# Two hybrid layers on one core: the second 512 columns of gate and up computed directly, the seven-product accumulators moved to one PSUM pool and read by ScalarE, other SBUF slots, the row sums of x ranked late

## The chip, the cores and the metric

The kernel runs on 1 core of one Trainium2 chip. The metric is the device time of one execution in microseconds (us). The kernel before has a median of 2263.99 us over 3 runs (2261.82 to 2264.88). Engines are named as in the profile: PE is TensorE, DVE VectorE, ACT ScalarE, POOL GpSimd, SP the queue that starts nearly all transfers.

## What is computed

Two layers over 256 tokens with a model width of 2048, in fp32. Each layer adds three things to x: a mixer (a state-space half and a latent-attention half), a cross-attention to a memory, and a gated MLP. The change lies in the MLP, with its norm in front:

```
h = rms_norm(x, ffn_norm_g[l])
x = x + swiglu(h, w_gate[l], w_up[l], w_down[l])
def swiglu(h, w_gate, w_up, w_down):
    return (jax.nn.silu(h @ w_gate) * (h @ w_up)) @ w_down    # 2048 -> 5632 -> 2048
```

## The kernel before, in words

**Exact products from two parts.** A weight arrives as a raw unit of 256 rows by 512 columns (512 KB, a tile of 128x1024). `split_w` makes two parts of it: `hi`, the raw number rounded to the fast fp32 format (a CAST, on ACT as a rule), and `lo`, the rest (a subtraction on DVE). The rows of x are split the same way. A product then takes three matmuls: x hi with weight lo, x hi with weight hi, x lo with weight hi. Nothing but these makes the work of DVE and ACT so large. All instructions are issued from one place, so the profile's rows all bear line 374, and tiles tell them apart.

**The MLP.** Its 5632 hidden columns are taken in eleven chunks of 512, in sections [0], [1,2], [3,4], and so on to [9,10]. For each chunk gate and up are computed, silu(gate) times up is formed in the tiles `gg`/`hh`, and it is turned by a transposing transfer (`split_T_dma`, `turn`) into the parts `hTh`, `hTl`. After each chunk of a section, `down` runs half of the output columns for the section before (48 or 96 matmuls), into `acc` tiles that `add_x` adds to x on DVE.

Chunk 0 is computed directly: `gemm` over the four quarters of the 2048 rows, for gate and then for up, 96 matmuls of 512 columns each, so 192. All other chunks go through `gate_up`. It combines the two token blocks, two parts of the rows and the pair gate/up as two-by-two block matrices and forms them with seven block products in place of eight (the quarter x1, rows 512 to 1023, stays direct). The products need sums of x's blocks (`s1` to `s4`, made once per layer in `seven_rows`) and sums of weights (`add(b11, b11, b12)` and such, on DVE; `plus` adds one more by an accumulating transfer on POOL's queue). In each chunk that is 7 times 18 plus 48 = 174 matmuls, 25 units to split where the direct way has 16, 10 sums of raw units on DVE and 2 accumulating transfers.

**Banks and slots.** The eight PSUM banks are two pools of four: `acc` (the gemms) and `tp` (transposes and small work). `gate_up` takes its first two accumulators, `q` and `f`, from `acc` and the other two, `cg` and `cu`, from `tp`; `down` takes its two per 512 output columns from `acc` too. In SBUF, 20 slots of the pool `w` hold raw, hi and lo units, 22 slots `b4` hold the parts of x, hT and their kin, 6 slots `s2` hold small tiles.

**Who sets the order.** Nothing is written to an engine at once. A recorder takes all instructions with a rank (place in the program plus `rec.bias`: smaller goes first), and `issue` then plays a list schedule with its own costs, engine by engine, picking the one that can start first and among those the lowest rank; slots are given out in that play as well. The chip runs the resulting order, each engine strictly in its own. Splits have a bias of -400, the sums `add` of -425, `add_x` none.

Of the kernel before, what the change touches and what calls it, by code (L numbers as in the profile page):

```python
# [17 lines left out]
P = 128  # L18
# [359 lines left out]
def hybrid_kernel(ctx: ExitStack, tc: tile.TileContext, const, vec, rows, x_in, x_tr, mem, mem_tr, positions, w_in, w_q_b,  # L378
# [110 lines left out]
    def load_unit(w, r0, c0, n, pieces=1):  # L489

        if not ahead and not asked:
            return ask(w, r0, c0, n, pieces)
        key = id(w), r0, c0
        while key not in asked or (ahead and len(asked) <= 2):
            first = ahead.pop(0)
            asked[id(first[0]), first[1], first[2]] = ask(*first, 512)
        return asked.pop(key)

    def load_raw(w, r0, c0, n, pieces=1):

        return [load_unit(w, r0 + 256 * h, c0, n, pieces) for h in range(2)]

    def ask(w, r0, c0, n, pieces=1):
        raw = wpool.tile([P, 2, n], F32, tag="w", name=nm("raw"), bufs=20)
        src = w[r0:r0 + 256, c0:c0 + n].rearrange("(k p) n -> p k n", p=P)
        for i in range(pieces):
            k = slice(2 // pieces * i, 2 // pieces * (i + 1))
            SP.dma_start(raw[:, k, :], src[:, k, :])
        return raw
# [116 lines left out]
    def norm_chunk_whole(j, ssx, g, by_dma=False):  # L626

        x_squares(j, ssx)
        xg = b4([P, 4, S], "xg")
        if by_dma:  # L630
            turn(lambda t: x[j][:, t, :], xg.rearrange("p b s -> p (b s)"))
            for b in range(4):
                copy(xg[:, b, :], xg[:, b, :], g[:, 4 * j + b:4 * j + b + 1])
            return xg
        for pair in range(2):
            ps = tp_tile().rearrange("p (b s) -> p b s", b=2)
            for i in range(2):
                b = 2 * pair + i
                for t in range(NT):
                    T.transpose(ps[:, i, t * P:(t + 1) * P], x[j][:, t, b * P:(b + 1) * P], ident)  # L640
                copy(xg[:, b, :], ps[:, i, :], g[:, 4 * j + b:4 * j + b + 1])
        return xg

    def seven_rows(xa, xb, n):


        a = {f"a{t + 1}{i + 1}": src[:, :, t * P:(t + 1) * P] for i, src in enumerate((xa, xb)) for t in range(NT)}
        if n == 4:
            sums = [b4([P, 2, 4, P], "xs") for _ in range(2)]
            tmp = [sums[i // 2][:, i % 2] for i in range(4)]  # L650
        else:
            sums = b4([P, 4, 2, P], "xs")
            tmp = [sums[:, i] for i in range(4)]
        out, room = {}, []
        for name in ("a11", "a12", "a22", "a21", "s1", "s2", "s3", "s4"):
            if name[0] == "s":
                a[name] = tmp[int(name[1]) - 1]
                do, u, v = {"s1": (V.tensor_sub, "a21", "a22"), "s2": (V.tensor_sub, "s1", "a11"),
                            "s3": (V.tensor_sub, "a11", "a21"), "s4": (V.tensor_add, "a12", "s2")}[name]
                do(a[name], a[u], a[v])  # L660
            if n == 4:
                d = b4([P, 2, 4, P], "x7", F32R)
            else:
                if not room:
                    both = b4([P, 2, 2, 2, P], "x7", F32R)
                    room = [both[:, 0], both[:, 1]]
                d = room.pop(0)
            copy(d[:, 0], a[name])
            V.tensor_sub(d[:, 1], a[name], d[:, 0].bitcast(F32))
            out[name] = d  # L670
        return out

    def load_T(src, j, g, name, pieces=1):
# [486 lines left out]
    def mem_T(l):  # L1160
# [10 lines left out]
        rec.after = None  # L1171
        return mT

    def add_x(j, accs):
        for t in range(NT):
            xs = x[j][:, t, :]
            V.tensor_add(xs, xs, accs[t])

    mixer_end, hidden_end = [None], [None]

# [120 lines left out]
            src = w[r0 + 256 * h:r0 + 256 * (h + 1), c0:c0 + 512].rearrange("(k p) n -> p k n", p=P)  # L1301
            G.dma_start(raw[h], src, accum_op=ALU.add)

    def add(out, a, b, do=V.tensor_add):
        rec.bias -= 425
        for o, u, v in zip(out, a, b) if isinstance(out, list) else [(out, a, b)]:
            do(o, u, v)
        rec.bias += 425

    def gate_up(wg, wu, c, x1, half, full, rstd):  # L1310

        c0 = 512 * c
        q, f = acc_tile(), acc_tile()
        cg, cu = tp_tile(), tp_tile()
        gg, uu = b4([P, NT, 512], "gg"), [s2([P, 512], "uu") for _ in range(NT)]  # L1320

        def product(acc, d, raw, start=False, stop=False):
            parts = split_w(raw)
            order = [(h, k, i) for h in range(len(parts)) for k, i in ((0, 1), (1, 1), (0, 0), (0, 2), (1, 0), (1, 2))]
            for m, (h, k, i) in enumerate(order):
                T.matmul(acc, d[:, i // 2, 2 * h + k, :], parts[h][i % 2][:, k, :], start=start and m == 0,
                         stop=stop and m == len(order) - 1, skip_group_check=True)

        b11 = load_raw(wg, 1024, c0, 512)
        product(q, full["a11"], b11, start=True)  # L1330
        h11 = load_unit(wg, 0, c0, 512)
        product(q, half["a11"], [h11])
        A.copy(gg[:, 0, :], q)

        b12 = load_raw(wu, 1024, c0, 512)
        add(b11, b11, b12)
        product(f, full["s1"], b11, start=True)
        h12 = load_unit(wu, 0, c0, 512)
        add(h11, h11, h12)
        product(f, half["s1"], [h11])  # L1340
        A.copy(uu[0], f)

        b22 = load_raw(wu, 1536, c0, 512)
        add(b11, b11, b22)
        add(b12, b12, b22)
        product(cu, full["s4"], b22, start=True)
        h22 = load_unit(wu, 256, c0, 512)
        add(h11, h11, h22)
        add(h12, h12, h22)
        product(cu, half["s4"], [h22])  # L1350
        product(q, full["s2"], b11)
        plus(b11, wg, 1536, c0)
        product(q, half["s2"], [h11])
        add(uu[0], uu[0], q, V.tensor_sub)

        b21 = load_raw(wg, 1536, c0, 512)
        product(cg, full["a12"], b21, start=True)
        h21 = load_unit(wg, 256, c0, 512)
        add(h11, h11, h21)
        product(cg, half["a12"], [h21])  # L1360
        product(q, full["s3"], b12)
        product(q, half["s3"], [h12])
        mm_chunk([cu, f], x1, load_w(wu, 512, c0, 512), 512, [False] * NT, [True, True], again=True)
        A.copy(uu[1], f)
        add(uu[1], uu[1], q, V.tensor_sub)
        add(uu[0], uu[0], cu)
        mm_chunk([cg, q], x1, load_w(wg, 512, c0, 512), 512, [False] * NT, [True, False], again=True)
        add(gg[:, 0, :], gg[:, 0, :], cg)
        A.activation(gg[:, 0, :], gg[:, 0, :], AF.Silu, scale=rstd[:, 0:1])

        product(q, full["a22"], b11)
        product(q, half["a22"], [h11], stop=True)
        A.activation(gg[:, 1, :], q, AF.Silu, scale=rstd[:, 1:2])
        for t in range(NT):
            V.scalar_tensor_tensor(gg[:, t, :], uu[t], rstd[:, t:t + 1], gg[:, t, :], op0=ALU.mult, op1=ALU.mult)
        return gg

    def ffn(l, xT, rstd):
# [18 lines left out]
        sections, before = [[0], [1, 2], [3, 4], [5, 6], [7, 8], [9, 10]], None  # L1397
        for sec in sections:
            for i, c in enumerate(sec):
                if c == 0:  # L1400
                    ahead.extend((w, r + h, 0) for w in (wg, wu) for r in FULL for h in (0, 256))
                else:
                    ahead.extend((w, r, 512 * c) for w, r in (
                        (wg, 1024), (wg, 1280), (wg, 0), (wu, 1024), (wu, 1280), (wu, 0), (wu, 1536), (wu, 1792),
                        (wu, 256), (wg, 1536), (wg, 1792), (wg, 256), (wu, 512), (wu, 768), (wg, 512), (wg, 768)))
                if before:
# [6 lines left out]
        for sec in sections:  # L1413
            hT = []
            for i, c in enumerate(sec):
                if c == 0:
                    xs = [lambda i, k, t: half[f"a{t + 1}{1 + k // 2}"][:, i, k % 2, :], x1]
                    xs += [lambda i, k, t, b=b: full[f"a{t + 1}{b}"][:, i, k, :] for b in (1, 2)]
                    ag = gemm(xs, wg, FULL, 0, 512)
                    hh = b4([P, NT, 512], "gg")  # L1420
                    for t in range(NT):
                        A.activation(hh[:, t, :], ag[t], AF.Silu, scale=rstd[:, t:t + 1])
                    au = gemm(xs, wu, FULL, 0, 512)
                    for t in range(NT):
                        V.scalar_tensor_tensor(hh[:, t, :], au[t], rstd[:, t:t + 1], hh[:, t, :], op0=ALU.mult,
                                               op1=ALU.mult)
                else:
                    hh = gate_up(wg, wu, c, x1, half, full, rstd)
                hc = chunk_T("hT")
                split_T_dma(hc, lambda t: hh[:, t, :], None, hh.rearrange("p t (u s) -> p (t u) s", s=S), (A, V))  # L1430
                hT.append(hc)
                if before:
                    n = DC // len(sec)
# [88 lines left out]
```

## Time and profile before

| | |
|---|---|
| median of 3 runs | 2263.99 us |
| the profiled execution | 2267.05 us, its span 2265.3 us |
| granted TensorE clock, mean | 0.997 |
| PE busy in the span | 2222.9 us (98%) |
| DVE / ACT busy | 1910.6 us (84%) / 1500.4 us (66%) |
| HBM read | 450.92 MB |

The MLP of the first layer runs on PE from about 434 to 1131 us, that of the second from about 1561 to 2262 us. In the page's 40 slices PE is below 9 tenths in two alone, which begin at 510 and 1642 us; DVE is at 9 or more tenths in most slices of the two MLPs.

### The profile page before, as it was taken

The numbers are of one execution on the slowest core, as the hardware profiler recorded it, in microseconds if no ns is written. First come the engines' busy times: TensorE is split into PE (matmuls) and PEld (weight loads), VectorE is DVE, ScalarE is ACT, GpSimd is POOL, SyncE is SP. The second block draws the span as 40 slices with busy tenths as digits, with TensorE's granted clock in tenths as the row PEclk, the third lists the DMA queues.
The fourth block names the chain that finished last, engine by engine and source line by source line (L and its number), as shares of the span: only waits on it lengthen the run. The fifth ranks groups of instructions, "written<-read, shape, count | busy, mean of one in ns | idle before, by whom it ended". The sixth has DMA issues, their size and how long they took to land.

```text
span 2265.3 us, 29133 instructions
## 1 busy us (share of the span) xinstructions
PE 2222.9 (98%) x10118; PEld 1845.7 (81%) x10118; DVE 1910.6 (84%) x2568; ACT 1500.4 (66%) x2183; POOL 93.0 (4%) x78
## 2 busy tenths in 40 slices
PE   9999999998999999999999999999989999999999
PEld 9878878787888888888898788887878888888787
DVE  7898876789998999999778888857899999999894
ACT  7768666766766666676666686657666667666762
POOL 0001000000000000000000010000000000000000
PEclk9999999999999999999999999999999999999999
DMA  9866496676777777787777665856767777777773
GB/s 319 236 193 186 142 284 196 187 212 197 239 224 212 229 232 235 228 247 226 194 230 223 172 177 171 244 185 182 219 201 226 232 220 213 236 231 226 239 234 138
DMA packets 374515, 487.96 MB, mean 215 GB/s; under 512 B 145376, under 2 KB 168544, under 8 KB 374368
## 3 DMA queue, kind: packets, MB, share of 16 engines
q1 hardware_dynamic: 363456, 465.13, 65.1%
q0 software_dynamic: 10912, 20.98, 5.5%
q8 instruction: 79, 1.29, 0.2%
q14 instruction: 68, 0.56, 0.1%
HBM read 450.92 MB, written 2.10 MB: 200 GB/s over the span
## 4 chain that ended last, share of the span: by engine, by line
PE 71%; DVE 6%; DMA 5%; issue 2%; ACT 1%; SPq 0%; DVEq 0%; ACTq 0%
PE acc L374 59%; PE tp L374 13%; DVE lo L374 3%; DMA raw<-in_w_up_dram 1%; DVE raw L374 1%; DMA ht<-hs 1%; ACT hi L374 1%; DVE x L374 1%; DMA raw<-in_w_xv_dram 0%; DMA raw<-in_w_out_dram 0%; DMA raw<-in_w_in_dram 0%; DVE uu L374 0%; DMA raw<-in_w_gate_dram 0%; SPq L374 0%; DVE hTl L374 0%
## 5 line engine op out<-in xcount | busy, mean ns | idle before, releaser
L374 ACT CAST hi<-raw 128x1024 fp32r<-128x1024 f32 (+3 forms) x996 | 1002.7, 1034 | 559.9 <-PE acc L374 223.4
L374 DVE TENSOR_TENSOR lo<-raw,hi 128x1024 fp32r<-128x1024 f32 (+3 forms) x998 | 1167.9, 1200 | 177.3 <-ACT hi L374 125.2
L374 PE MATMUL acc<-hi,x 128*128 128x512 f32 x1392 | 373.1, 392 | 0.0
L374 PEld LDWEIGHTS acc<-hi,x 128*128 128x128 f32 x1392 | 263.4, 189 | 55.4
L374 PE MATMUL acc<-hi,xTh 128*128 128x512 f32 (+1 forms) x768 | 289.3, 377 | 0.0
L374 PE MATMUL acc<-hi,xTl 128*128 128x512 f32 (+1 forms) x768 | 289.1, 376 | 0.0
L374 DVE TENSOR_TENSOR raw<-raw,raw 128x1024 f32<-128x1024 f32 x200 | 239.2, 1221 | 50.7 <-DMA raw<-in_w_up_dram 50.2
L374 PE MATMUL acc<-hi,hTh 128*128 128x512 f32 x704 | 273.9, 389 | 0.0
L374 PE MATMUL acc<-hi,hTl 128*128 128x512 f32 x704 | 273.9, 389 | 0.0
L374 PE MATMUL acc<-lo,x 128*128 128x512 f32 x696 | 214.8, 394 | 13.2 <-DVE x L374 13.2
L374 PE MATMUL acc<-lo,xTh 128*128 128x512 f32 (+1 forms) x768 | 211.7, 378 | 6.0 <-DVE uu L374 4.2
L374 PE MATMUL acc<-lo,hTh 128*128 128x512 f32 x704 | 191.2, 390 | 1.3 <-DVE lo L374 1.3
L374 PEld LDWEIGHTS acc<-lo,xTh 128*128 128x128 f32 x768 | 140.6, 188 | 31.3 <-DVE uu L374 6.8
L374 PEld LDWEIGHTS acc<-lo,x 128*128 128x128 f32 x696 | 131.1, 190 | 42.5 <-DVE x L374 14.9
L374 PEld LDWEIGHTS acc<-hi,xTh 128*128 128x128 f32 x768 | 144.8, 189 | 23.2 <-issue 0.7
L374 PEld LDWEIGHTS acc<-hi,xTl 128*128 128x128 f32 x768 | 144.7, 188 | 23.1 <-issue 0.7
L374 PEld LDWEIGHTS acc<-lo,hTh 128*128 128x128 f32 x704 | 131.8, 188 | 30.1 <-DVE lo L374 3.0
L374 PEld LDWEIGHTS acc<-hi,hTh 128*128 128x128 f32 x704 | 132.1, 188 | 27.5
L374 PEld LDWEIGHTS acc<-hi,hTl 128*128 128x128 f32 x704 | 132.1, 188 | 27.4
L374 PE MATMUL tp<-hi,x 128*128 128x512 f32 x480 | 128.6, 390 | 0.0
L374 DVE TENSOR_TENSOR x<-x,acc 128x512 f32<-128x512 f32 x128 | 83.5, 682 | 32.5 <-PE acc L374 32.4
L374 PEld LDWEIGHTS tp<-hi,x 128*128 128x128 f32 x480 | 90.1, 188 | 19.2
(306 smaller groups left out, 2781.7 us busy)
## 6 DMA issues: line engine op xcount, KB each, us to landing
raw<-in_w_gate_dram SPq DMA_DIRECT2D x176, 512.0 KB, 4.9
raw<-in_w_up_dram SPq DMA_DIRECT2D x176, 512.0 KB, 4.5
raw<-in_w_down_dram SPq DMA_DIRECT2D x176, 512.0 KB, 5.4
raw<-in_w_in_dram SPq DMA_DIRECT2D x80, 512.0 KB, 4.4
raw<-in_w_out_dram SPq DMA_DIRECT2D x64, 512.0 KB, 4.5
raw<-in_w_gate_dram POOLq DMA_DIRECT2D x40, 512.0 KB, 7.5
raw<-in_w_in_dram SPq DMA_DIRECT2D x46, 368.0 KB, 4.5
raw<-in_w_kv_b_dram SPq DMA_DIRECT2D x16, 512.0 KB, 3.9
```

The lines of the kernel that those rows point to most:

```text
L374: fn(*args, **kw)
```

## The change

Five edits. (1) Chunk 1 is computed directly like chunk 0, so `gate_up` runs 9 times in a layer. (2) In `gate_up` all four accumulators come from `tp`. ACT copies `q` out after the second and the third product that end in it, where DVE subtracted it from a copy of `f` made earlier; DVE then subtracts that copy from `f` in its bank. The product of `s4` with `b22` stands ahead of the two sums that read `b22`. (3) Other slots: `gg` and `hh` are two `s2` tiles each, the turned words go to a `b4` tile of their own (`whole`) and not back into `gg`, and the raw units of rows 0 to 255 (`h11`, `h12`) take `b4` slots and not `w` slots. (4) The four sums of x's blocks rank 300 later, and in `norm_chunk_whole` the transposes of a pair come before its two copies. (5) `add_x` gets the bias of -425. The diff, cut to its core:

```diff
-    def ask(w, r0, c0, n, pieces=1):
-        raw = wpool.tile([P, 2, n], F32, tag="w", name=nm("raw"), bufs=20)
+    def ask(w, r0, c0, n, pieces=1, other=False):
+        raw = b4([P, 2, n], "raw") if other else wpool.tile([P, 2, n], F32, tag="w", name=nm("raw"), bufs=20)
...
@@ seven_rows
         for name in ("a11", "a12", "a22", "a21", "s1", "s2", "s3", "s4"):
+            if name == "s1":
+                rec.bias += 300
...
+        rec.bias -= 300
         return out
...
     def add_x(j, accs):
         for t in range(NT):
             xs = x[j][:, t, :]
-            V.tensor_add(xs, xs, accs[t])
+            add(xs, xs, accs[t])
...
@@ gate_up
-        q, f = acc_tile(), acc_tile()
-        cg, cu = tp_tile(), tp_tile()
-        gg, uu = b4([P, NT, 512], "gg"), [s2([P, 512], "uu") for _ in range(NT)]
+        q, f, cg, cu = (tp_tile() for _ in range(4))
+        gg, uu = [[s2([P, 512], n) for _ in range(NT)] for n in ("gg", "uu")]
...
         product(f, half["s1"], [h11])
-        A.copy(uu[0], f)
 
         b22 = load_raw(wu, 1536, c0, 512)
+        product(cu, full["s4"], b22, start=True)
         add(b11, b11, b22)
         add(b12, b12, b22)
-        product(cu, full["s4"], b22, start=True)
         h22 = load_unit(wu, 256, c0, 512)
+        product(cu, half["s4"], [h22])
         add(h11, h11, h22)
         add(h12, h12, h22)
-        product(cu, half["s4"], [h22])
         product(q, full["s2"], b11)
         plus(b11, wg, 1536, c0)
         product(q, half["s2"], [h11])
-        add(uu[0], uu[0], q, V.tensor_sub)
+        A.copy(uu[0], q)
+        add(uu[0], f, uu[0], V.tensor_sub)
...
         product(q, half["s3"], [h12])
+        A.copy(uu[1], q)
         mm_chunk([cu, f], x1, load_w(wu, 512, c0, 512), 512, [False] * NT, [True, True], again=True)
-        A.copy(uu[1], f)
-        add(uu[1], uu[1], q, V.tensor_sub)
+        add(uu[1], f, uu[1], V.tensor_sub)
         add(uu[0], uu[0], cu)
         mm_chunk([cg, q], x1, load_w(wg, 512, c0, 512), 512, [False] * NT, [True, False], again=True)
...
@@ ffn
-                if c == 0:
+                if c < 2:
...
-                    ag = gemm(xs, wg, FULL, 0, 512)
-                    hh = b4([P, NT, 512], "gg")
+                    ag = gemm(xs, wg, FULL, 512 * c, 512)
+                    hh = [s2([P, 512], "gg") for _ in range(NT)]
...
-                split_T_dma(hc, lambda t: hh[:, t, :], None, hh.rearrange("p t (u s) -> p (t u) s", s=S), (A, V))
+                split_T_dma(hc, lambda t: hh[t], None, None, (A, V))
```

The first place is PE's queue in the first layer where the first half of `down` (`hTh`, `hTl` into `acc`) ends and the next `gate_up` begins with its product of `a11` (here the tile `x_841`) into `q`. Before (the next chunk is number 2):

```order
L374 MATMUL acc_5074<-hi_4984,hTl_4980 128x512
L374 MATMUL acc_5076<-hi_4984,hTh_4805 128x512
L374 MATMUL acc_5076<-hi_4984,hTl_4980 128x512
L374 MATMUL acc_5124<-lo_5027,x_841_4421 128x512 x2
L374 MATMUL acc_5124<-hi_5000,x_841_4421 128x512 x4
```

And now, at the same place of the program:

```order
L374 MATMUL acc_5049<-hi_4928,hTl_4798 128x512
L374 MATMUL acc_5057<-hi_4928,hTh_4786 128x512
L374 MATMUL acc_5057<-hi_4928,hTl_4798 128x512
L374 MATMUL tp_5087<-lo_4958,x_841_4404 128x512 x2
L374 MATMUL tp_5087<-hi_4946,x_841_4404 128x512 x4
```

What was `acc_5124`, a fifth tile on the four banks that `down` fills, is now `tp_5087` on a bank that `down` never uses.

The second place is DVE's queue around the same point, with the sums `x<-x,acc` of `add_x` that empty `down`'s banks (`x_215` and `x_302` are the first two column quarters of x). Before:

```order
L374 TENSOR_TENSOR raw_4952<-raw_4952,raw_5046 128x1024
L374 TENSOR_TENSOR raw_5002<-raw_5002,raw_5046 128x1024
L374 SCALAR_TENSOR_TENSOR gg_4733<-uu_4847,rx_y_4548,gg_4733 128x512
L374 TENSOR_TENSOR lo_5112<-raw_4991,hi_5102 128x1024
L374 TENSOR_TENSOR raw_4957<-raw_4957,raw_5096 128x1024
L374 TENSOR_TENSOR raw_5019<-raw_5019,raw_5096 128x1024
L374 SCALAR_TENSOR_TENSOR gg_4733<-uu_4959,rx_y_4548,gg_4733 128x512
L374 TENSOR_TENSOR x_215<-x_215,acc_5035 128x512
L374 TENSOR_TENSOR x_215<-x_215,acc_5037 128x512
L374 TENSOR_TENSOR x_302<-x_302,acc_5074 128x512
L374 TENSOR_TENSOR x_302<-x_302,acc_5076 128x512
```

And now:

```order
L374 TENSOR_TENSOR raw_4705<-raw_4705,raw_4972 128x1024
L374 SCALAR_TENSOR_TENSOR gg_4860<-acc_4862,rx_y_4377,gg_4860 128x512
L374 TENSOR_TENSOR lo_5023<-raw_4900,hi_5013 128x1024
L374 TENSOR_TENSOR raw_4936<-raw_4936,raw_4999 128x1024
L374 TENSOR_TENSOR raw_4900<-raw_4900,raw_4999 128x1024
L374 TENSOR_TENSOR x_215<-x_215,acc_5008 128x512
L374 TENSOR_TENSOR x_215<-x_215,acc_5011 128x512
L374 TENSOR_TENSOR lo_5059<-raw_4915,hi_5035 128x1024
```

The first pair of sums of x stood behind two rounds of weight sums and both products with up; it now stands behind one split and two weight sums, and the second pair no longer follows it at once.

The third place is PE's queue in the same `gate_up`, where the direct quarter (`xTh`, `xTl`) of up ends and that of gate goes on in `q`. Before, in chunk 2, two matmuls of the next `down` stand between:

```order
L374 MATMUL tp_5238<-hi_5320,xTh_4340 128x512
L374 MATMUL tp_5238<-hi_5320,xTl_4352 128x512
L374 MATMUL acc_5410<-lo_5383,hTh_4805 128x512
L374 MATMUL acc_5414<-lo_5383,hTh_4805 128x512
L374 MATMUL acc_5124<-lo_5333,xTh_4340 128x512 x2
L374 MATMUL acc_5124<-hi_5308,xTh_4340 128x512
```

And now, with `f` in `tp_5120`, `cu` in `tp_5157`, `cg` in `tp_5227` and `q` in `tp_5087`:

```order
L374 MATMUL tp_5157<-hi_5254,xTl_4391 128x512
L374 MATMUL tp_5120<-hi_5254,xTh_4383 128x512
L374 MATMUL tp_5120<-hi_5254,xTl_4391 128x512
L374 MATMUL tp_5227<-lo_5287,xTh_4383 128x512
L374 MATMUL tp_5087<-lo_5287,xTh_4383 128x512
L374 MATMUL tp_5227<-hi_5267,xTh_4383 128x512
```

The quarter for `cg` and `q` follows at once and takes both token blocks in turn, where before `cg` was done alone, then `q`. Over the whole program PE gets 36 more matmuls of 512 columns, DVE 18 fewer splits and 20 fewer sums of raw units, ACT 28 fewer casts, and POOL 4 fewer accumulating transfers. In the mixers and the output projections no engine's order changes.

## Rows read from the trace of the kernel before

**Rows 1.** The page, busy time of each engine over the span.

```profile
PE 2222.9 (98%) x10118; PEld 1845.7 (81%) x10118; DVE 1910.6 (84%) x2568; ACT 1500.4 (66%) x2183; POOL 93.0 (4%) x78
```

**Rows 2.** Stretches of both MLPs: length, busy us of PE, PEld, DVE, ACT, POOL, PEclk.

```profile
434.00:530.00 96.00, 94.83 (x424) 77.78 (x423) 84.74 (x95) 64.93 (x86) 4.20 (x3) 1.00 0.66 201
530.00:552.00 22.00, 16.36 (x61) 12.92 (x60) 17.87 (x19) 13.05 (x15) 1.98 (x2) 0.84 0.56 165
552.00:1131.00 579.00, 573.83 (x2518) 471.47 (x2517) 522.78 (x524) 388.33 (x438) 20.68 (x18) 1.00 0.75 227
1561.00:1657.00 96.00, 94.85 (x422) 77.34 (x422) 84.40 (x95) 64.72 (x85) 4.17 (x3) 1.00 0.66 202
1657.00:1679.00 22.00, 16.29 (x62) 12.97 (x61) 18.33 (x20) 13.12 (x15) 1.85 (x2) 0.84 0.57 163
1679.00:2262.00 583.00, 575.27 (x2522) 471.95 (x2520) 508.90 (x488) 369.98 (x404) 19.93 (x17) 1.00 0.72 222
```

**Rows 3.** PE's waits, first layer's MLP: for whom, total us, times, longest us.

```profile
PE acc L374 <- DVE x L374: 6.0, 2, 5.6
PE tp L374 <- DVE lo L374: 2.2, 4, 1.2
PE acc L374 <- DVE uu L374: 1.7, 3, 0.7
PE tp L374 <- DVE x L374: 1.2, 1, 1.2
```

**Rows 4.** PE's waits, second layer's MLP.

```profile
PE acc L374 <- DVE x L374: 7.2, 2, 5.7
PE tp L374 <- DVE lo L374: 2.6, 3, 1.2
PE acc L374 <- DVE uu L374: 2.5, 3, 1.3
```

**Rows 5.** PE in order of time, first layer: start, us, what, [idle before].

```profile
537.22 1.22 PE L374 MATMUL acc<-lo,x 128*128 128x512 f32 x2 [5.64 <-DVE x L374]
...
543.15 1.07 PE L374 MATMUL acc<-hi,x 128*128 128x512 f32 x4
```

**Rows 6.** The same place in the second layer.

```profile
1664.70 1.22 PE L374 MATMUL acc<-lo,x 128*128 128x512 f32 x2 [5.71 <-DVE x L374]
...
1669.68 0.63 PE L374 MATMUL acc<-lo,x 128*128 128x512 f32 x2
```

**Rows 7.** DVE in order of time during the first layer's wait.

```profile
533.55 2.36 DVE L374 TENSOR_TENSOR raw<-raw,raw 128x1024 f32<-128x1024 f32 x2
535.82 0.75 DVE L374 SCALAR_TENSOR_TENSOR gg<-uu,rx_y,gg 128x512 f32<-128x512 f32 x1
536.48 2.48 DVE L374 TENSOR_TENSOR x<-x,acc 128x512 f32<-128x512 f32 x4
```

**Rows 8.** The chain that ended last: start, us, what; a product's 18 matmuls.

```profile
604.86 4.08 PE acc L374 x18
```

**Rows 9.** Groups of the first MLP, DVE, by form: count, busy us, mean ns, idle before.

```profile
L374 DVE TENSOR_TENSOR lo<-raw,hi 128x1024 fp32r<-128x1024 f32 x347 | 408.7, 1220 | 26.8 <-ACT hi L374 17.4 <-PE acc L374 6.0 <-issue 1.1
L374 DVE TENSOR_TENSOR raw<-raw,raw 128x1024 f32<-128x1024 f32 x100 | 119.7, 1221 | 25.3 <-DMA raw<-in_w_up_dram 25.1
```

**Rows 10.** The same of ACT.

```profile
L374 ACT CAST hi<-raw 128x1024 fp32r<-128x1024 f32 x345 | 350.0, 1051 | 184.5 <-PE acc L374 98.6 <-DMA raw<-in_w_up_dram 34.7 <-DMA raw<-in_w_down_dram 22.6
```

**Rows 11.** SP in order of time, loads ahead of chunk 4.

```profile
629.82 2.59 SPq L374 DMA_DIRECT2D raw<-in_w_gate_dram  x3
...
639.24 3.00 SPq L374 DMA_TRANSPOSE ht<-hs  x1
```

**Rows 12.** PE in order of time, chunk 4's first product.

```profile
653.65 0.61 PE L374 MATMUL acc<-lo,x 128*128 128x512 f32 x2
```

**Rows 13.** The page, transfers: issuer, count, size, median us to landing.

```profile
raw<-in_w_gate_dram SPq DMA_DIRECT2D x176, 512.0 KB, 4.9
```

**Rows 14.** PE in order of time, one wait for the subtraction from `uu`, second layer.

```profile
1878.40 0.73 PE L374 MATMUL acc<-lo,xTh 128*128 128x512 f32 x2 [1.06 <-DVE uu L374]
```

More of the change, by code (lines that the diff above doesn't have):

```diff
@@ L495, in load_unit @@
             first = ahead.pop(0)
-            asked[id(first[0]), first[1], first[2]] = ask(*first, 512)
+            asked[id(first[0]), first[1], first[2]] = ask(*first[:3], 512, 1, first[3:])
         return asked.pop(key)
@@ L640, in norm_chunk_whole @@
                     T.transpose(ps[:, i, t * P:(t + 1) * P], x[j][:, t, b * P:(b + 1) * P], ident)
+            for i in range(2):
+                b = 2 * pair + i
                 copy(xg[:, b, :], ps[:, i, :], g[:, 4 * j + b:4 * j + b + 1])
@@ L1172, in mem_T, with add @@
         return mT
+    def add(out, a, b, do=V.tensor_add):
+        rec.bias -= 425
+        for o, u, v in zip(out, a, b) if isinstance(out, list) else [(out, a, b)]:
+            do(o, u, v)
+        rec.bias += 425
     def add_x(j, accs):
@@ L1302, in plus @@
             G.dma_start(raw[h], src, accum_op=ALU.add)
[L1304 to L1308, printed above, removed]
     def gate_up(wg, wu, c, x1, half, full, rstd):
         c0 = 512 * c
-        q, f = acc_tile(), acc_tile()
-        cg, cu = tp_tile(), tp_tile()
-        gg, uu = b4([P, NT, 512], "gg"), [s2([P, 512], "uu") for _ in range(NT)]
+        q, f, cg, cu = (tp_tile() for _ in range(4))
+        gg, uu = [[s2([P, 512], n) for _ in range(NT)] for n in ("gg", "uu")]
         def product(acc, d, raw, start=False, stop=False):
@@ L1332, in gate_up @@
         product(q, half["a11"], [h11])
-        A.copy(gg[:, 0, :], q)
+        A.copy(gg[0], q)
         b12 = load_raw(wu, 1024, c0, 512)
@@ L1362, in gate_up @@
         product(q, half["s3"], [h12])
+        A.copy(uu[1], q)
         mm_chunk([cu, f], x1, load_w(wu, 512, c0, 512), 512, [False] * NT, [True, True], again=True)
-        A.copy(uu[1], f)
-        add(uu[1], uu[1], q, V.tensor_sub)
+        add(uu[1], f, uu[1], V.tensor_sub)
         add(uu[0], uu[0], cu)
         mm_chunk([cg, q], x1, load_w(wg, 512, c0, 512), 512, [False] * NT, [True, False], again=True)
-        add(gg[:, 0, :], gg[:, 0, :], cg)
-        A.activation(gg[:, 0, :], gg[:, 0, :], AF.Silu, scale=rstd[:, 0:1])
+        add(gg[0], gg[0], cg)
+        A.activation(gg[0], gg[0], AF.Silu, scale=rstd[:, 0:1])
         product(q, full["a22"], b11)
         product(q, half["a22"], [h11], stop=True)
-        A.activation(gg[:, 1, :], q, AF.Silu, scale=rstd[:, 1:2])
+        A.activation(gg[1], q, AF.Silu, scale=rstd[:, 1:2])
         for t in range(NT):
-            V.scalar_tensor_tensor(gg[:, t, :], uu[t], rstd[:, t:t + 1], gg[:, t, :], op0=ALU.mult, op1=ALU.mult)
+            V.scalar_tensor_tensor(gg[t], uu[t], rstd[:, t:t + 1], gg[t], op0=ALU.mult, op1=ALU.mult)
         return gg
@@ L1399, in ffn @@
             for i, c in enumerate(sec):
-                if c == 0:
-                    ahead.extend((w, r + h, 0) for w in (wg, wu) for r in FULL for h in (0, 256))
+                if c < 2:
+                    ahead.extend((w, r + h, 512 * c) for w in (wg, wu) for r in FULL for h in (0, 256))
                 else:
-                    ahead.extend((w, r, 512 * c) for w, r in (
+                    ahead.extend((w, r, 512 * c) + ((1,) if r == 0 else ()) for w, r in (
                         (wg, 1024), (wg, 1280), (wg, 0), (wu, 1024), (wu, 1280), (wu, 0), (wu, 1536), (wu, 1792),
@@ L1415, in ffn @@
             for i, c in enumerate(sec):
-                if c == 0:
+                if c < 2:
                     xs = [lambda i, k, t: half[f"a{t + 1}{1 + k // 2}"][:, i, k % 2, :], x1]
                     xs += [lambda i, k, t, b=b: full[f"a{t + 1}{b}"][:, i, k, :] for b in (1, 2)]
-                    ag = gemm(xs, wg, FULL, 0, 512)
-                    hh = b4([P, NT, 512], "gg")
+                    ag = gemm(xs, wg, FULL, 512 * c, 512)
+                    hh = [s2([P, 512], "gg") for _ in range(NT)]
                     for t in range(NT):
-                        A.activation(hh[:, t, :], ag[t], AF.Silu, scale=rstd[:, t:t + 1])
-                    au = gemm(xs, wu, FULL, 0, 512)
+                        A.activation(hh[t], ag[t], AF.Silu, scale=rstd[:, t:t + 1])
+                    au = gemm(xs, wu, FULL, 512 * c, 512)
                     for t in range(NT):
-                        V.scalar_tensor_tensor(hh[:, t, :], au[t], rstd[:, t:t + 1], hh[:, t, :], op0=ALU.mult,
+                        V.scalar_tensor_tensor(hh[t], au[t], rstd[:, t:t + 1], hh[t], op0=ALU.mult,
                                                op1=ALU.mult)
```

## Prediction

> **What bounds the kernel now.** I read the page first. PE is busy for 98% of the span [rows 1], so time can be won only where PE stands idle or runs slowly, and every added matmul costs its full length. The change lies in the two MLPs, so next come the stretches: in the first MLP PE is busy for 94.83 + 16.36 + 573.83 of 697 us, in the second for 94.85 + 16.29 + 575.27 of 701 [rows 2], so it idles for 12.0 and 14.6 us, 26.6 in all. The reader is to see that 5.64 + 5.71 of these fall into two stretches of 22 us at the same place of both layers, the only ones with a granted clock under 1.00.
>
> The waits say for whom. Nearly all is DVE: 6.0 and 7.2 us for sums into x, 2.2 and 2.6 for `lo` parts, 1.7 and 2.5 for `uu` [rows 3, 4]. In order of time the large one is a single wait, 5.64 us in the first layer, 5.71 in the second, at the first product of a `gate_up` that follows half a `down` [rows 5, 6]. Its matmul goes into an `acc` tile. Its operands are not what is late: the releaser is the sum of `down`'s result into x, so it waits for a bank. DVE shows why it comes late: the four sums of x start at 536.48, behind raw sums and the last product of the chunk before [rows 7], and PE goes on at 537.22. PE then runs at about half its pitch: 14 matmuls take 543.15 - 537.22 = 5.93 us and in the second layer 12 take 4.98 [rows 5, 6], 0.42 us each, where 18 take 4.08 elsewhere, 0.2267 each [rows 8]. That is the lower of the two levels, 1.2 and 2.4 GHz, after PE had stood still.
>
> **The change part by part.**
>
> Chunk 1 direct: 192 matmuls in place of 174, 18 more per layer, 36 in all. At 0.2267 us [rows 8] that is +8.2 us, all of it on PE and hidden by nothing.
> The Trainium skill (TensorE: Matmul & The Clock Gate, Back-to-back issue gap) puts a lone warm matmul of 512 columns at 216 ns, less in a stream; the row here has 227, so by that figure the term would be at most 7.8, and the measured pitch decides.
>
> The same edit takes work from the others: 18 splits and 20 raw sums off DVE, 38 times 1.22 us = 46 us [rows 9], less ten casts and ten copies that the planner now gives to DVE, and 28 casts off ACT, 29 us [rows 10]. Neither engine ends anything by itself, so I count this at nothing; it is cover, since DVE is busy for 523 of 579 us in the long stretch [rows 2], and less work there makes the waits for `lo` rarer.
>
> All four accumulators from `tp`: the first product of a `gate_up` no longer needs a bank that `down` has filled. PE's queue shows `tp_5087` where `acc_5124` stood. So the waits for x on an `acc` tile go: 6.0 + 7.2 = 13.2 us [rows 3, 4]. With the pause goes the stretch at half pitch behind it: 5.93 - 14 times 0.2267 = 2.8 us and 4.98 - 12 times 0.2267 = 2.3 us [rows 5, 6, 8]. Together -18.2. What could be late next at that place is the bank of a `tp` tile; the last `gate_up` has given all of them back by the 48 matmuls of `down` between, 10.9 us, when the DVE sums with -425 come first.
>
> ACT reads `q` halfway: before, `q` was free for the quarter x1 of gate only after `f` was complete, ACT had copied `f` and DVE had subtracted `q`, with nothing between on PE but stray matmuls. Now ACT copies `q` right after the third product, and 24 matmuls of x1 (5.4 us) into `cu` and `f` lie between. So PE's waits for `uu` go, 1.7 + 2.5 = 4.2 us [rows 3, 4], of which one is 1.06 us long [rows 14]. The copy stands in ACT's queue behind casts; ACT often waits there for PE itself [rows 10], and these casts belong to later matmuls, so I see no circle. Without the 5.4 us of cover it would cost about what it cost before.
>
> `s4` with `b22` ahead of the two sums: the waits of PE for `lo` into a `tp` tile, 2.2 + 2.6 = 4.8 us [rows 3, 4], stand mostly at the third product, whose `lo` parts came behind four raw sums of 1.22 us. The edit takes these from in front. Bounds: nothing and -4.8. DVE stays nearly full from chunk 2 on, so I take half, -2.4.
>
> Slots: two raw units of each chunk no longer take a `w` slot, so loads can run a little further ahead; `whole` and the two small `gg` tiles move copies to other slots without adding any. But loads into `b4` wait their turn among hT's pieces: in SP's queue `h11` now stands behind the transposing transfer of the chunk before. In the trace that transfer is issued at 639.24 for 3.00 us [rows 11], a load lands 4.9 us after its issue [rows 13], a cast and a split take 2.3 [rows 9, 10], which gives 649.4; PE begins the chunk at 653.65 [rows 12] and needs `h11` 12 matmuls later, at 656.4. So 7 us of slack, and I count it at nothing.
>
> `add_x` early, sums of x late, transposes of a pair together: at the MLP's start PE waits for x before a transpose, 1.2 us in each layer [rows 3]. The x sums for these transposes now stand earlier on DVE, but so do the transposes on PE. Bounds -2.4 and +2.4; I take 0.
>
> A new wait: the first half `down` after chunk 1 finds the `acc` banks held by the direct chunk. PE's queue takes its second output quarter in turns of five matmuls, the second tile on the bank that the first sum of x gives back, and on DVE that sum stands behind a split and two raw sums, 3.7 us [rows 9]. They must be done within the 24 matmuls (5.4 us) of the first quarter, and raw sums there have waited for loads from up [rows 9]. I take 1.5 us per layer, +3.0; bounds 0 and the old wait, 5.7 with its 2.5 of slow pitch per layer, +16.4.
>
> The sum: 8.2 - 18.2 - 4.2 - 2.4 + 3.0 = -13.6 us. The profiled execution took 2267.05 us (1.75 of it around its span), so it would become 2253.4. The median shown is 2263.99, 3.1 below the profiled one; I give the prediction against it: 2250.4 us. No change means within 0.2%, 2259.5 to 2268.5, about what a measurement of this kernel can tell.
>
> **The rivals.**
>
> Better: all of the waits for `lo` and at the start go, and no new one comes: another -2.4 - 2.4 - 3.0, so 2242.6. For it: PE's queue is in plain program order from chunk 4 on. Against: DVE is still some nine tenths full.
>
> The bank wait moves: the first half `down` waits for the sums of x as long as the product after it did. +16.4 in place of +3.0 gives -0.2: 2263.8, no change. For it: the same sums on the same in-order engine behind raw sums that wait for loads. Against: DVE has just had a chunk with 16 splits and no raw sum in 43.5 us of PE, so it should not be behind.
>
> Slower: `h11` comes late. SP is in order and its load takes a `b4` slot; if the slot or the transfer ahead holds it for more than the 7 us of slack, PE stands at the 13th matmul of `gate_up`, 9 times in each layer. At 1.5 us beyond the slack that is +27, so +13.4: 2277. For it: 22 slots hold x's fourteen pieces and up to eight of hT. Against: the slack, and the loads are asked for early.
>
> Slower by the clock: `gate_up` now cycles through four banks of one pool with short pauses; if a pause in each of the 18 were followed by a half-pitch stretch that loses 2.5 us as in [rows 5, 6], it would cost 45 us: 2295. Against: the wait of 1.06 us left no such stretch [rows 14], and the clock is 1.00 over 579 and 583 us in which four `acc` and `tp` tiles already take turns [rows 2].
> The Trainium skill (TensorE: Matmul & The Clock Gate, A second HAM failure mode: psum-queue depth-cycling) tells of a kernel in which such cycling made the clock fall and rise again; no stretch of this trace shows it.
>
> **How the numbers follow.** The forecast 0.60, with its own range 2244 to 2257 (the -4.8 or 0 for `lo`, 0 to 6 for the new wait, 2.4 either way at the start, not all at once); better 0.14; the bank wait moved 0.15, of which 0.04 moves in part only and still gains more than 0.2%; `h11` late 0.08, of which 0.02 stays within 0.2%; the clock 0.03. Faster: 0.60 + 0.14 + 0.04 = 0.78. Within 0.2%: 0.10 + 0.02 = 0.12. Slower: 0.01 + 0.06 + 0.03 = 0.10. For 8 in 10 the range goes from 2242 to 2262: the forecast, most of the better case and the near part of the moved wait.
>
> **What would show it.** Right: 36 more matmuls at an unchanged pitch; no wait of PE for x of more than 2 us in either MLP; the granted clock at 1.00 in every stretch of 22 us there; PE's waits for `uu` gone; PE idle in the two MLPs down from 26.6 us to some 10. Wrong: a wait for x inside the first half `down` of 5 us; waits for `lo` from gate's raw units at the 13th matmul of each `gate_up`; waits for ACT's `uu` at the quarter of gate; or an MLP whose idle time fell and whose pitch rose.

## The result, and the profile after

The changed kernel has a median of 2248.77 us (2247.6 to 2251.41, 4 runs) where the kernel before had 2263.92 (2261.82 to 2264.88, 4 runs) on the same chip: a ratio of 0.9936, 95% interval 0.9919 to 0.9953, so 15.2 us less where 13.6 were forecast. The profiled execution took 2247.70 us. It is 1.1 below its median where the one of before was 3.1 above, so the two traces differ by 19.4 us.

The page after, busy time of each engine [rows 1]:

```profile
PE 2222.8 (99%) x10154; PEld 1853.0 (83%) x10154; DVE 1878.5 (84%) x2538; ACT 1461.0 (65%) x2143; POOL 87.9 (4%) x74
```

PE is busy for as long as before with 36 matmuls more. The stretches of the two MLPs after, cut at about the same places in the program as [rows 2] and with the same columns (the last two are the busy share of the DMA engines and GB/s), and below them two stretches of 22 us in the first:

```profile
435.00:530.00 95.00, 95.00 (x425) 78.71 (x424) 65.26 (x75) 54.33 (x73) 1.07 (x1) 1.00 0.66 198
530.00:552.00 22.00, 22.00 (x98) 18.21 (x98) 21.68 (x21) 15.21 (x16) 2.45 (x2) 1.00 0.71 174
552.00:1128.00 576.00, 572.15 (x2518) 471.93 (x2517) 525.14 (x532) 378.79 (x430) 20.11 (x17) 1.00 0.76 229
1552.00:1648.00 96.00, 96.00 (x429) 79.55 (x428) 66.33 (x76) 54.48 (x72) 2.20 (x1) 1.00 0.64 195
1648.00:1670.00 22.00, 22.00 (x99) 18.22 (x98) 21.68 (x21) 14.16 (x15) 2.42 (x2) 1.00 0.77 205
1670.00:2242.00 572.00, 567.21 (x2489) 467.27 (x2488) 504.77 (x486) 359.22 (x394) 19.23 (x16) 1.00 0.72 223
```

```profile
588.00:610.00 22.00, 19.66 (x86) 15.91 (x85) 22.00 (x20) 15.56 (x18) 2.37 (x2) 0.98 0.84 238
610.00:632.00 22.00, 22.00 (x93) 18.08 (x92) 17.80 (x20) 15.70 (x20) 0.00 (x0) 0.94 0.76 205
```

The two stretches that had a granted clock of 0.84 and 5.64 + 5.71 us of idle time are full now, at 1.00. All idle time of PE, 3.85 + 4.79 = 8.6 us, lies in the long stretches. PE's waits in the first MLP after, then in the second (for whom, total us, times, longest us), against [rows 3, 4]:

```profile
PE tp L374 <- DVE lo L374: 3.2, 2, 2.3
PE tp L374 <- DVE x L374: 0.5, 1, 0.5
```

```profile
PE tp L374 <- DVE lo L374: 4.8, 4, 2.9
```

The waits for x on an `acc` tile and those for `uu` are gone. What is left is for `lo`, and the largest in each layer is new. DVE and PE in order of time show first that the old place is free (the sums of x are over at 535.9, where they began at 536.48 in [rows 7], and `gate_up` follows on `down` at once, where [rows 5] had 5.64 us), then the new wait, with a cast close by (ACT in order of time):

```profile
528.88 1.29 DVE L374 TENSOR_TENSOR x<-x,acc 128x512 f32<-128x512 f32 x2
...
534.62 1.28 DVE L374 TENSOR_TENSOR x<-x,acc 128x512 f32<-128x512 f32 x2
...
602.09 8.03 DVE L374 TENSOR_TENSOR lo<-raw,hi 128x1024 fp32r<-128x1024 f32 x7
```

```profile
534.34 0.39 PE L374 MATMUL acc<-hi,hTl 128*128 128x512 f32 x1
534.57 0.61 PE L374 MATMUL tp<-lo,x 128*128 128x512 f32 x2
...
607.90 0.73 PE L374 MATMUL tp<-lo,xTh 128*128 128x512 f32 x2 [2.34 <-DVE lo L374]
...
609.56 1.06 PE L374 MATMUL tp<-lo,xTh 128*128 128x512 f32 x2
610.41 0.63 PE L374 MATMUL tp<-hi,xTh 128*128 128x512 f32 x1
```

```profile
606.12 1.05 ACT L374 CAST hi<-raw 128x1024 fp32r<-128x1024 f32 x1 [3.32 <-DMA raw<-in_w_gate_dram]
```

This is the first matmul of the quarter x1 in chunk 3, that of up, and what it waits for is DVE itself: DVE is busy for all of the 22 us from 588 on, and the seven splits from 602.09 on stand back to back. The cast beside it, which waits 3.32 us for a load from gate, is not in the way: it ends at 607.17, and the split that PE waited for, which ends just before 607.90 and takes 1.2 us, had begun by then. PE then spends 0.42 us on a matmul from 609.56 on, as after the old wait, but it lasts for a few matmuls only: the next 22 us hold 93 where a full stretch holds 97.

Of the forecast's 36 matmuls the chain that ended last shows the pitch unchanged: 288 matmuls in 65.29 us, 0.2267 each, as in [rows 8].

```profile
2176.78 65.29 PE acc L374 x288
```

The account of the traces goes by the starts of the matmuls, from the first of an MLP to its last. This time fell by 18.8 us in the two MLPs together (697.46 and 699.76 before, 688.44 and 689.93 after). What PE spent in it beyond 0.2267 us for each matmul of 512 columns fell from 42.9 to 15.9 us. Before, 25.9 of it was idle time of the waits, 4.9 the half pitch behind the two long ones, and 12.1 the rest (transposes of x that stand among the matmuls, a slow first matmul behind each wait, pauses too short to be listed). After, it is 8.0 idle, 3.1 at half pitch, and 4.8 the rest. So: -17.9 idle, -1.8 half pitch, -7.3 the rest, +8.2 for 36 matmuls.

### The profile page after: what moved, and what is told of

Its sections match the earlier page's. It is cut to its first block, busy times and chain, and to the rows that moved or that the text cites. A ratio compares the mean times of both kernels' runs of the same rounds, so it can differ in the third digit from the quotient of the medians.

```text
span 2245.9 us, 29023 instructions
## 1 busy us (share of the span) xinstructions
PE 2222.8 (99%) x10154; PEld 1853.0 (83%) x10154; DVE 1878.5 (84%) x2538; ACT 1461.0 (65%) x2143; POOL 87.9 (4%) x74
## 5 line engine op out<-in xcount | busy, mean ns | idle before, releaser
L374 ACT CAST hi<-raw 128x1024 fp32r<-128x1024 f32 (+2 forms) x968 | 973.8, 1033 | 564.4 <-PE acc L374 171.3
L374 PE MATMUL tp<-hi,x 128*128 128x512 f32 x1512 | 403.0, 389 | 0.0
L374 PEld LDWEIGHTS tp<-hi,x 128*128 128x128 f32 x1512 | 283.8, 188 | 59.3
L374 PE MATMUL acc<-hi,xTl 128*128 128x512 f32 (+1 forms) x640 | 239.0, 374 | 0.0
L374 PE MATMUL acc<-hi,xTh 128*128 128x512 f32 (+1 forms) x640 | 238.9, 374 | 0.0
L374 PE MATMUL tp<-lo,x 128*128 128x512 f32 x756 | 232.8, 390 | 2.9 <-DVE lo L374 2.8
L374 PEld LDWEIGHTS tp<-lo,x 128*128 128x128 f32 x756 | 141.0, 188 | 35.1 <-DVE lo L374 4.0
L374 PE MATMUL acc<-lo,xTh 128*128 128x512 f32 (+1 forms) x640 | 162.4, 374 | 2.3 <-DVE lo L374 2.3
L374 PE MATMUL tp<-hi,xTh 128*128 128x512 f32 x288 | 113.0, 393 | 0.0
L374 PE MATMUL tp<-hi,xTl 128*128 128x512 f32 x288 | 112.9, 393 | 0.0
```

The costliest lines, as they stand in the source:

```text
L374: fn(*args, **kw)
```

## The experiments

My theory was that of the forecast: the wait for x hangs on the bank, so the common pool removes it; the direct chunk costs its matmuls and is cover. The rival: the wait only shows that DVE runs late, so anything that relieves or reorders DVE ends it, and time is won only if DVE or the loads that it waits for become earlier. All ratios are against the kernel before on the same chip. It took 2274.5 to 2275.1 us on the three chips used here, 2263.9 on the one of the result. Every edit makes `issue` plan the MLPs anew, so a difference holds the new order of the engines along with the edit itself.

**Chunk 1 by seven products again** (all else as changed), twice, and the changed kernel once more beside the second:

```diff
-                if c < 2:
+                if c < 1:
```

> The changed kernel with chunk 1 by the seven products again, all other edits kept. Theory (the gain is the bank that gate_up no longer shares with down): 36 matmuls fewer, -8.2 us against the changed kernel, and the 5.6 us waits for x stay away, so about 2241 us, up to 2248 if DVE comes late for lo parts in chunk 1. Rival (the gain is the work taken off DVE by the direct chunk): DVE is late again at the start of both MLPs, by 8 us or more in each layer, so 2257 or more and PE waiting for lo or raw sums between 480 and 560 us.

> The changed kernel with chunk 1 by the seven products, again, beside the changed kernel on one chip. Theory now (the 36 matmuls are a plain cost and chunk 1 needs no help once the banks and the order of the sums are changed): 8 us below the changed kernel, both MLPs together 8 us shorter, about 2241. Rival (the earlier difference of 3 us was the chip's): within 2 us of the changed kernel.

> The changed kernel again, beside the next run on one chip. Both theories: 2246 to 2252 us, some 15 below the kernel before; PE waiting in the two MLPs for some 8 us, nearly all for lo.

Measured: 2245.86 us, 0.9871 (0.9855 to 0.9887); again 2243.69, 0.9859 (0.9841 to 0.9878); the changed kernel beside the latter 2251.29, 0.9895 (0.9879 to 0.9910). That was the theory's forecast each time; the changed kernel itself lies 23.2 us below the kernel before on that chip, where some 15 were expected. So the direct chunk costs 7.6 us, which is the 36 matmuls at 8.2 and nothing for its cover. The version without it beats both kernels, by 7.6 us the changed one and by 30.8 us the kernel before on that chip. PE's waits in its first MLP:

```profile
PE tp L374 <- DVE lo L374: 2.4, 4, 1.3
PE acc L374 <- ACT hTh L374: 1.4, 1, 1.4
PE tp L374 <- ACT uu L374: 0.9, 1, 0.9
```

The single wait of 2.3 us and more has gone from it as well. DVE is busier (1917.9 us over the program, 1878.3 in the changed kernel beside it), and in the traces the two MLPs are 8.2 us shorter (1370.6 against 1378.8), the 36 matmuls: PE loses no more time than in the changed kernel.

**Each of three edits alone on the kernel before.** The direct chunk:

```diff
-                if c == 0:
+                if c < 2:
...
-                    ag = gemm(xs, wg, FULL, 0, 512)
+                    ag = gemm(xs, wg, FULL, 512 * c, 512)
```

> The kernel before with chunk 1 direct and nothing else. Theory: q and f still share the four acc banks with down, the wait for x stays or shrinks a little, and 36 matmuls come on top: 2264 + 8 = 2272, at the least 2262. Rival: with DVE unloaded the sums of x are in time, the wait and the half-pitch stretch behind it go (-18) and 8 come on top: 2254.

Measured: 2261.93 us, 0.9945 (0.9934 to 0.9957), though it adds the same 36 matmuls; the rival's 10 us came, and more. The long wait before `gate_up` is gone, though `q` still comes from `acc`; the longest wait for x in the first MLP is 2.0 us and stands inside a later `down`, at 587.29:

```profile
PE acc L374 <- DVE uu L374: 2.1, 3, 1.1
PE acc L374 <- DVE x L374: 2.0, 1, 2.0
```

So the work that the direct chunk takes off DVE and ACT is worth 13.1 + 8.2 us in the old kernel, and nothing any more once the other edits are in.

The banks from one pool, with ACT's copies of `q`:

```diff
-        q, f = acc_tile(), acc_tile()
-        cg, cu = tp_tile(), tp_tile()
+        q, f, cg, cu = (tp_tile() for _ in range(4))
...
-        A.copy(uu[0], f)
...
-        add(uu[0], uu[0], q, V.tensor_sub)
+        A.copy(uu[0], q)
+        add(uu[0], f, uu[0], V.tensor_sub)
...
```

The same is done for `uu[1]`.

> The kernel before with all four accumulators of gate_up from tp and q copied out by ACT, nothing else (chunk 1 by seven products, sums of x's blocks and sums into x ranked as before). Theory: the waits for x on an acc tile (13.2), the half pitch behind them (5.0) and the waits for uu (4.2) go: 2264 - 22 = 2242, or up to 2250 if the wait comes back as one for lo. Rival: the wait only changes its name, DVE being behind at chunk 1 and 2: 2260 or more.

Measured: 2263.08 us, 0.9951 (0.9938 to 0.9964): 12.0 us, between theory and rival, where the forecast gave the same edit 22.4. The long wait ended, and waits for `lo` took part of its place (PE's waits, first MLP, then second, against 2.2 and 2.6 in [rows 3, 4]):

```profile
PE tp L374 <- DVE lo L374: 5.7, 6, 1.8
...
PE acc L374 <- DVE x L374: 1.2, 1, 1.2
```

```profile
PE tp L374 <- DVE lo L374: 6.9, 7, 3.2
```

The early sums into x, with the banks as before:

```diff
+            rec.bias -= 425
             V.tensor_add(xs, xs, accs[t])
+            rec.bias += 425
```

> The kernel before with the bias of -425 on the sums into x and nothing else. Theory now (the long wait was the late place of these sums on DVE, and any one of three edits ends it): the two waits of 5.6 us for x and the half pitch behind them go, 2264 - 12 to - 18 = 2246 to 2252, or somewhat less as waits for lo take a part of it, 2257. Rival (the shared bank itself is what matters): waits for x of 3 us or more stay at the gate_up after the first half down, 2260 to 2266.

> The kernel before once more with a profile, on the chip of the three runs beside it. Both theories: the two waits of 5.6 us for x with the half pitch behind them, PE losing some 40 us in the two MLPs; if it takes 2275 us and not 2264, the profile shows in which stretch the 11 us lie.

Measured: 2273.94 us, 0.9999 (0.9986 to 1.0013). The kernel before, traced on the same chip, took 2277.13. PE's waits over the whole program, first in the kernel before, then with the early sums:

```profile
PE acc L374 <- DVE x L374: 13.6, 4, 6.2
PE tp L374 <- DVE lo L374: 6.6, 8, 1.9
...
PE acc L374 <- DVE lo L374: 4.4, 4, 2.9
PE acc L374 <- DVE uu L374: 4.2, 5, 1.3
```

```profile
PE tp L374 <- DVE lo L374: 12.3, 15, 1.7
PE acc L374 <- DVE lo L374: 7.3, 8, 2.9
PE acc L374 <- DVE uu L374: 7.2, 9, 1.8
```

Neither expectation came. All 13.6 us of waits for x on an `acc` tile are gone, against the rival above, and the median is the same, against the theory: the waits for `lo` and `uu` rose by 5.7 + 2.9 + 3.0 = 11.6. The two traces differ by 4.2 us, and their two MLPs by 5.2 (1402.4 to 1397.1), so by its traces the edit won some 5 us of those waits at the most, by the medians nothing. This is the clearest run of all for the rival of this section: the longest wait of the trace was removed and came back as many short ones. DVE had nearly the same work to do (1909.5 and 1915.1 us busy), in another order.

**The two pools again** in the changed kernel, and in the version with seven products:

```diff
-        q, f, cg, cu = (tp_tile() for _ in range(4))
+        q, f = acc_tile(), acc_tile()
+        cg, cu = tp_tile(), tp_tile()
```

> The changed kernel with q and f from acc again, all other edits kept (chunk 1 direct, ACT copies q, add_x early). Theory: the wait for x on an acc tile is back at the gate_up after the first half down, 2 to 6 us with a half-pitch stretch of 2.5 behind the longer ones: 2255 to 2265. Rival: the direct chunk and the early sums into x have the banks free in time: 2249, and no wait for x over 1 us.

> The changed kernel with chunk 1 by seven products and q and f from acc again; other edits kept. Theory (the bank pool matters where DVE is full and not where the direct chunk relieves it): waits of PE for x or lo on acc tiles come back at chunks 2 and 3, 5 to 10 us, ratio 0.989 to 0.991. Rival (early sums into x free the banks in time everywhere): within 3 us, 0.986 to 0.987.

Measured: 2252.68 us, 0.9905 (0.9891 to 0.9918), beside 0.9895 with one pool; and 2245.05, 0.9868 (0.9855 to 0.9881), beside 0.9859 and 0.9871. No difference that can be told. Neither has a wait for x on an `acc` tile in its MLPs; of the first, all that PE waited for 1 us or more in the first MLP:

```profile
PE tp L374 <- DVE lo L374: 2.7, 1, 2.7
PE acc L374 <- DVE lo L374: 1.1, 2, 1.0
```

These are the rivals' forecasts. So with the other edits in, the common pool does nothing that a difference of some 4 us between runs would show. The two also differ by the direct chunk alone, 0.9905 to 0.9868, the same cost a second time: 0.0037 of 2275 is 8.4 us.

**The raw units of `h11` and `h12` back in `w` slots**, in the version with seven products:

```diff
-                    ahead.extend((w, r, 512 * c) + ((1,) if r == 0 else ()) for w, r in (
+                    ahead.extend((w, r, 512 * c) for w, r in (
```

> The changed kernel with chunk 1 by seven products and the raw units of rows 0 to 255 back in w slots, other edits kept. Theory (with DVE nearly full, PE's waits for lo shrink because loads and splits can run two units further ahead): PE loses some 10 us more in the two MLPs, mostly waiting for lo and DVE for raw units from up, so a ratio to before of 0.990 against 0.986 with these slots. Rival (the order in gate_up does it): 0.986, losses in the MLPs as with the slots.

Measured: 2258.08 us, 0.9933 (0.9917 to 0.9949) against 0.9859 and 0.9871 with them in `b4`: 14 to 17 us for an edit that adds no instruction, in the direction of the theory and more of it. In the traces the two MLPs take 1382.4 us, against 1370.6 with the slots, so some 12 us lie where the edit works. In the rows by line and form over the whole program, DVE's sums of weights wait 41.9 us for loads from up here, and 25.8 in the version with the slots in `b4`:

```profile
L374 DVE TENSOR_TENSOR raw<-raw,raw 128x1024 f32<-128x1024 f32 x200 | 240.7, 1222 | 42.6 <-DMA raw<-in_w_up_dram 41.9
```

```profile
L374 DVE TENSOR_TENSOR raw<-raw,raw 128x1024 f32<-128x1024 f32 x200 | 239.1, 1219 | 26.4 <-DMA raw<-in_w_up_dram 25.8 <-DVE lo L374 0.2
```

So DVE stands still for these loads for 16 us more, and PE pays where DVE is behind. One such place, DVE and PE of the first MLP with the units in `w` slots, in order of time:

```profile
549.50 8.04 DVE L374 TENSOR_TENSOR lo<-raw,hi 128x1024 fp32r<-128x1024 f32 x7
```

```profile
556.46 0.73 PE L374 MATMUL tp<-lo,xTh 128*128 128x512 f32 x2 [2.64 <-DVE lo L374]
...
558.54 1.06 PE L374 MATMUL tp<-lo,xTh 128*128 128x512 f32 x2
```

PE waits 2.64 us for a split while DVE runs seven of them without a pause; behind it PE runs at half pitch. That the slots give this time through loads further ahead is what these rows fit; the plan differs between the two runs as well, and no run separates the two.

**The sums of weights ahead of `s4`'s product**, as before, in the version with seven products:

```diff
-        product(cu, full["s4"], b22, start=True)
         add(b11, b11, b22)
         add(b12, b12, b22)
+        product(cu, full["s4"], b22, start=True)
...
```

> The changed kernel with chunk 1 by seven products and the product of s4 with b22 behind the sums that read b22, as before; other edits kept. Theory (slots): within 3 us, ratio 0.986 to 0.987. Rival (order): the waits for lo into a tp tile at the third product are back, 5 to 10 us, ratio 0.988 to 0.990.

Measured: 2247.70 us, 0.9876 (0.9861 to 0.9890), 2 to 4 us above the two runs without it and inside their intervals. The time is inconclusive; the trace is not for the rival. PE waits for `lo` on `tp` tiles for 7.1 us over the program, where the two runs without the edit have 6.6 and 6.3, and the two long ones (2.64 and 2.66 us) stand before the quarter x1 of chunk 3, as in the changed kernel, and not at the third product.

**The planner's matmul cost set to the measured pitch**, an attempt at a faster version:

```diff
-            return max(passes * n / 2400 + 0.003, 0.107), self.LAG
+            return max(passes * n * 0.2267 / 512, 0.107), self.LAG
```

> The changed kernel with chunk 1 by seven products and, in the planner's costs, the measured pitch of 0.2267 us for a matmul of 512 columns in place of 0.2163. Theory (part of PE's waits comes from plans that run 5 per cent fast on PE, so that DVE stands waiting for PE with work behind it): PE loses 2 to 6 us less in the two MLPs, but other stages are planned anew too, so 2238 to 2248 with the same before at 2274, ratio 0.984 to 0.988. Rival (the plan's pitch does not matter): 0.986, losses in the MLPs as without it.

Measured: 2289.39 us, 1.0062 (1.0042 to 1.0082), slower by 43 to 46 us than the same kernel with the old cost, where both expectations had no loss. PE's waits over the whole program:

```profile
PE tp L374 <- DVE lo L374: 9.8, 5, 5.1
PE tp L374 <- DVE x L374: 8.1, 3, 4.6
PE tp L374 <- ACT uu L374: 7.8, 4, 3.6
```

Waits of 4 and 5 us appear, in stages that the change doesn't touch too: of the 42 to 44 us between the traces, half lie outside the two MLPs, where this edit alone of all changes most of the order. Why the order got worse with the truer cost stays open.

## Why the prediction was right, and what in it was not

The sum held: 13.6 us forecast, 15.2 measured. Its terms held less well, the errors cancelled, and that is luck: on another chip the same change gained 23.2 us. Of the five signs of being right, four came; the granted clock was not 1.00 in every stretch of 22 us (0.98 and 0.94 above).

*36 matmuls, +8.2.* Confirmed three times: the unchanged pitch, 7.6 us and 8.4 us.

*Its cover at nothing.* Right in the changed kernel; alone on the kernel before it is worth some 20 us, which no part of the working allowed for.

*All four accumulators from `tp`, -18.2.* The effect came: 13.2 us of waits and the half pitch behind them are gone. The pool is not needed for it: with the early sums or the direct chunk the wait goes without the common pool, and in the changed kernel taking the pool out again changes nothing that can be told. The step that failed is the price, that PE would win the length of the wait. With ACT's copies the pool won 12.0 us of 22.4 on the kernel before, and the early sums, which end the wait as well, won nothing: the waits for `lo` and `uu` behind it rose by 11.6 of 13.6 us.

*Waits for `uu`, -4.2.* Gone in the changed kernel; in the early-sums run, without ACT's copies, they grew.

*Waits for `lo`, -2.4 with 0 and -4.8 as bounds.* Wrong in sign. With `acc` and `tp` together they were 2.2 + 2.6 + 0.8 + 0.5 = 6.1 us in the MLPs and are 8.0 now, at another place (before the quarter x1 of chunk 3), with 3.1 us of half pitch behind them. DVE is busy without a pause there.

*The new wait in the first half `down`, +3.0.* It didn't come: PE is busy for all of the 22 us there.

*Start of the MLP at 0.* The two waits for x of 1.2 us became one of 0.5.

*Slots at nothing.* The largest miss. The 7 us of slack for `h11`, read at chunk 4, did not hold everywhere: in chunk 5 its load stands behind the transposing transfer, is issued at 707.61 for a chunk that PE begins at 711.68, and PE waits 0.87 us for its split (in the second layer 0.93 us, in chunk 7). That is little; but the gain of two more `w` slots a chunk was counted at nothing, and taking them away costs 12 to 17 us with seven products in chunk 1. The row that spoke for it stood in [rows 9]: 25.1 us of DVE's idle time ended by a load from up. It is 7.6 in the changed kernel's first MLP:

```profile
L374 DVE TENSOR_TENSOR raw<-raw,raw 128x1024 f32<-128x1024 f32 x90 | 107.4, 1218 | 7.7 <-DMA raw<-in_w_up_dram 7.6
```

Of the rivals none came. The better case had the waits for `lo` gone, and they stayed; the moved bank wait shows in no row, the late `h11` costs 1.8 us in place of 27, and the clock fell once in each MLP, behind the waits of 2.3 and 2.9 us, and not in each `gate_up`. The Trainium skill (TensorE: Matmul & The Clock Gate, A second HAM failure mode: psum-queue depth-cycling) tells of a kernel in which going through PSUM banks, with short idle times between groups of matmuls, made the clock fall and rise again. This trace shows no such thing: four banks of one pool take turns at a granted clock of 1.00 outside those two places.

Left open: why the gain is 0.64% on the chip of the result and 1.05% on another (intervals 0.9919 to 0.9953 and 0.9879 to 0.9910). The changed kernel takes nearly the same on both, 2248.77 and 2251.29 us; the kernel before differs by 10.6, spread over its whole trace (of 10.1 us between its two traces 5.1 lie in the MLPs). Without the slots and the direct chunk a gain of 0.67% is left, and the common pool adds nothing to it that can be told; how it divides among ACT's copies of `q`, the early sums into x and the rest isn't shown. The late sums of x's rows with the joined transposes, and the slots of `gg` and `whole`, weren't tried by themselves.

## What to carry to other kernels

When an in-order engine that is nine tenths full feeds the bound one, the longest wait in the list may be only where its lateness shows, and not what it costs: ask what the next few instructions wait for before its length goes into a sum. Edits that relieve the same engine don't add: the direct chunk gained 13 us alone and lost 8 beside the others, so after a bundle is in, take each edit out again. And a buffer slot has a price like an instruction: where the feeding engine's idle time ends with a load, count it.

## What was not expected of the hardware

The same program took 2263.9 us on one chip and 2274.5 to 2275.1 on three others, with a mean granted clock of 0.997 on the one (its traced execution) and 0.994 to 0.998 on the others; which part of the chip makes the 10.6 us isn't shown. And a single pause of PE of 2.3 us (607.90) is followed by matmuls of 0.42 us, the lower of the two levels, 1.2 and 2.4 GHz, where one of 1.06 us was not [rows 14]. The length of the pause alone doesn't settle it: at the same place of the run with two pools again, a pause of 2.71 us (609.39) is followed by matmuls of 0.23 us at a granted clock of 1.00, and in the run with the direct chunk alone one of 1.99 us (587.29) by matmuls of 0.43.
